# Moving two copies of a decoder step, the spread of a bias table and the carry-over of a convolution state, from the convolution into the first feed-forward block

## The chip, the core and the metric

The kernel runs on one core of one Trainium2 chip. The metric is device time in microseconds (us); of several runs the median is given. The profile is one execution taken by the hardware profiler; its times count from the first instruction of the span.

## What is computed

One inference step of a two-layer decoder: 512 prompt tokens and 64 sample tokens (8 sequences of 8), width 1024. Layer 0 mixes tokens with a convolution module, layer 1 with sliding-window attention that has a relative-position bias. Both layers then run a causal feed-forward block (width 2816, with a 3-tap convolution inside) and add a gated per-layer embedding.

```python
def _conv_module(xn, hist, ...):
    u = xn @ w_pw1 + b_pw1
    a, g = jnp.split(u, 2, axis=-1)
    u = a * jax.nn.sigmoid(g)
    uh = jnp.concatenate([hist.astype(u.dtype), u], axis=1)
    c = _dwconv_valid(uh, w_dw) + b_dw
    c = jax.nn.silu(_layernorm(c, ln_g, ln_b))
    return c @ w_pw2 + b_pw2, uh[:, -(CONV_K - 1):]
def _rel_bias(dist, table):
    vals = table[_t5_bucket(dist)].astype(jnp.float32)
    return jnp.moveaxis(vals, -1, 0).reshape(N_KV_HEADS, GROUP, *dist.shape)
```

Two small things in this matter here. The new convolution state of the 8 sample sequences is the last 30 rows of `uh`: 22 old rows, copied unchanged from `state_conv` (output `conv_old`, 704 KB), and 8 new ones. The bias of head h between two positions depends on their distance alone, so one row of 383 numbers for each of 16 heads holds all of it.

## The kernel before

The core goes through four stages in order: `conv_stage`, `ffn_stage(0)`, `att_stage`, `ffn_stage(1)`. Activations lie as 128 features by tokens. Tokens are handled in two parts, part 0 of 256 columns and part 1 of 320 (256 prompt, 64 sample). Every product is made of three matrix multiplications, high by high, high by low and low by high (`mm3`, lines 175 to 177). So each weight block of 128 x 1024 (512 KB) is loaded by a DMA of the SP queue into one of 3 `raw` buffers (line 216), rounded by ScalarE into `wh` (line 163), and VectorE, or for a few blocks GpSimd, makes the rest `wl` (line 166 or 223). In the feed-forward stage 8 pairs `wh`/`wl` are live (4 in `wp`, 4 in `w2`), and `ensure` runs up to 4 blocks ahead of use.

The order of work in the convolution is written out in the string `CONV`: `aM,P` is the first projection of block M, part P (`pw1`); `mM` regroups its result through DRAM (`regroup`, DMAs `d_u` and `x`), `cM,G` is a group of taps of the depthwise convolution as 18 multiplications (`taps`, lines 584 and 585), `bM` brings the result back through DRAM (`ungroup`, DMAs `d_c` and `h`), `oM` is the sample part on GpSimd (`taps_smp`, line 611 on). A group of taps has its own weights, 576 KB, loaded into one of two `traw` buffers (line 565, the first 12 on the GpSimd queue, the other 20 on SP's), rounded by ScalarE into `th`, the rest made by VectorE into `tl`. A scheduler may move instructions a little on each engine; those under `keep` stay in the order of the program.

`bias_table` makes the 16 rows of 383 numbers in the SBUF tile `ng` (16 partitions) and returns a function that spreads them: each row is written 128 times to `d_bias` in DRAM (16 x 128 x 383 numbers, 3064 KB), so that attention can later read it with a step of 382 and get the bias by distance (`bias_rows`, line 451). Entry `B` of `CONV`, in the middle of the convolution, calls this function (line 443) and issues the copy of `conv_old` (line 641), both on the GpSimd queue:

```python
elif kind == "B":
    bias_out()
    keep(nc.gpsimd.dma_start(out=o["conv_old"], in_=a["state_conv"][0][:, 8:30, :]))
```

In `ffn_stage` the list of `ffn_order` alternates `A` (up-projection of pair x, part 0), `B` (part 1) and the down-projections `DA`, `DB` of groups of pairs. In `up`, part 1 uses GpSimd for three small copies (lines 726, 727 and `stash`, line 732); products go to one of 6 PSUM banks (`bank`), which ScalarE and VectorE empty.

Of the kernel before, what the change touches and what calls it, by code (L numbers as in the profile page):

```python
# [9 lines left out]
F32 = mybir.dt.float32  # L10
# [7 lines left out]
P = 128  # L18
# [9 lines left out]
QSB = 5  # L28
LBUF = 4
CONV = """  # L30
X0 a0,0 X1 a1,0 a2,0 a0,1 m0 a1,1 m1 a3,0 o0 a2,1 m2 c0,0 a4,0 c0,1 c0,2 o1 a3,1 c0,3 b0 m3 c1,0 a5,0 c1,1 c1,2 o2 a4,1 c1,3 b1 m4 c2,0 a6,0 c2,1 c2,2 B
o3 a5,1 c2,3 b2 m5 c3,0 a7,0 c3,1 c3,2 o4 a6,1 c3,3 b3 m6 c4,0 c4,1 i0,0 o5 a7,1 c4,2 m7 c4,3 b4 c5,0 i0,1 c5,1 c5,2 P c5,3 b5 o6 c6,0 p0,0 c6,1 c6,2 c6,3
b6 o7 c7,0 i1,0 c7,1 c7,2 c7,3 b7 p0,1 i1,1 L0 p1,0 L1 M0 p1,1 w0,0 w1,0 M1 w0,1 w2,0 w1,1 w3,0 n0 w2,1 r0 w3,1 n1 r1
"""
# [121 lines left out]
class Trunk:  # L156
# [273 lines left out]
    def bias_table(self, sp):  # L430

        nc, a = self.nc, self.a
        tab = sp.tile([32, 16], F32, tag="tab", name="tab", bufs=1)
        nc.scalar.dma_start(out=tab, in_=a["rel_bias"])
        oh = sp.tile([32, 384], F32, tag="pst", name="oh")
        nc.scalar.dma_start(out=oh, in_=a["c_onehot"])
        ng = sp.tile([16, 384], F32, tag="ng", name="ng", bufs=1)
        nc.scalar.dma_start(out=ng, in_=a["c_neg"])
        ps = self.bank("bps", st=True)
        self.T.matmul(ps[0:16, :384], lhsT=tab, rhs=oh, start=True, stop=True)  # L440
        self.V.tensor_tensor(out=ng, in0=ps[0:16, :384], in1=ng, op=ALU.add)
        self.d_bias = self.drp.tile([16, P, 383], F32, name="d_bias")
        return lambda: self.tc.keep_in_program_order(nc.gpsimd.dma_start(out=self.d_bias, in_=ng[:, 0:383].unsqueeze(1).to_broadcast([16, P, 383])))

    def bias_rows(self, out, h0, nh, nq, ns):

# [36 lines left out]
    def conv_stage(self):  # L483
        nc, tc, a, o = self.nc, self.tc, self.a, self.o
# [13 lines left out]
        self.d_pp = {(l, p): self.drp.tile([P, KD, PN[p]], F32, name=f"d_pp{l}{p}") for l in range(2) for p in PARTS}  # L498
        with tc.tile_pool(name="w2c", bufs=2) as w2, tc.tile_pool(name="cvp", bufs=2) as sp:
            self.phase("conv", w2)  # L500
            bias_out = self.bias_table(sp)
            cc = self.h
            us, norms = {}, {}
            keep = tc.keep_in_program_order
            x = sp.tile([P, 4, 136], F32, tag="x", name="x", bufs=1)
# [7 lines left out]
            def pw1(m, part):  # L513

                n = PN[part]
                if part == 0:
                    us[m] = sp.tile([P, 816], F32, tag="u", name="u", bufs=UB)
                    keep(nc.sync.dma_start(out=us[m][:, 512:], in_=a["sc"][m]))
                u = us[m]
                wa, wg = self.wcols(("pw1", m, 0)), self.wcols(("pw1", m, 1))  # L520
                pg = self.bank("pg")
                self.lin(pg[:, :n], wg, part)
                pa = self.bank("pa")
                self.lin(pa[:, :n], wa, part)
                sg = sp.tile([P, 320], F32, tag="sg", name="sg")
                self.V.tensor_tensor(out=sg[:, :n], in0=pg[:, :n], in1=self.Rx[part], op=ALU.mult)
                self.V.tensor_tensor(out=pa[:, :n], in0=pa[:, :n], in1=self.Rx[part], op=ALU.mult)
                self.sig = self.A.activation(out=sg[:, :n], in_=sg[:, :n], func=AF.Sigmoid, bias=self.col["b_pw1"][:, 8 + m:9 + m], scale=1.0)
                ba = self.col["b_pw1"][:, m:m + 1]
                uq = u[:, 0:512].rearrange("p (r q) -> p q r", r=4)[:, part * 64:part * 64 + 64]  # L530
                q4 = lambda t: t[:, 0:256].rearrange("p (q r) -> p q r", r=4)
                self.V.scalar_tensor_tensor(out=uq, in0=q4(pa), scalar=ba, in1=q4(sg), op0=ALU.add, op1=ALU.mult)
                if part:
                    self.done(("pw1", m, 0), ("pw1", m, 1))
                    self.V.scalar_tensor_tensor(out=smp(u, 30, 8), in0=pa[:, 256:320].rearrange("p (b t) -> p b t", b=8), scalar=ba, in1=sg[:, 256:320].rearrange("p (b t) -> p b t", b=8), op0=ALU.add, op1=ALU.mult)
# [3 lines left out]
            def u_out(i):  # L539
                keep(nc.gpsimd.tensor_copy(out=ucat[:, i, 0:32].rearrange("p (r q) -> p r q", r=4), in_=us[i][:, 0:512].rearrange("p (r q) -> p r q", r=4)[:, :, 120:128]))  # L540
                keep(nc.gpsimd.tensor_copy(out=ucat[:, i, 32:96].rearrange("p (b t) -> p b t", b=8), in_=smp(us[i], 30, 8)))
                if i == KD - 1:
                    keep(nc.gpsimd.dma_start(out=o["conv_new"], in_=ucat))
# [47 lines left out]
            def ungroup(m):  # L591

                v = vs.pop(m)
                for r in range(4):
                    nc.sync.dma_start(out=d_c[m][:, :, r].rearrange("g c j -> c g j"), in_=v[32 * r:32 * r + 32])
                dv = d_c[m].rearrange("g c r j -> (g c) r j")
                for part in PARTS:
                    nc.sync.dma_start(out=cc[part][:, m, 0:256].rearrange("p (r j) -> p r j", r=4), in_=dv[:, :, part * 64:part * 64 + 64])
# [23 lines left out]
            for e in CONV.split():  # L622
                kind, v = e[0], [int(d) for d in e[1:].split(",") if d]
                if kind == "X":
                    self.norm_x(v[0], sp)
                elif kind == "a":
                    pw1(*v)
                elif kind == "s":
                    pass
                elif kind == "o":  # L630
                    taps_smp(*v)
                    u_out(*v)
                elif kind == "m":
                    regroup(*v)
                elif kind == "c":
                    taps(*v)
                elif kind == "b":
                    ungroup(*v)
                elif kind == "B":
                    bias_out()  # L640
                    keep(nc.gpsimd.dma_start(out=o["conv_old"], in_=a["state_conv"][0][:, 8:30, :]))
                elif kind == "P":
                    dm = self.smp.tile([P, 1], F32, tag="rs_t", name="dm")
                    self.after(self.A.activation(out=dm, in_=self.zero[:, 0:1], func=AF.Silu), self.sig)
                elif kind == "L":
                    norms[v[0]] = self.ln_y(part_c(v[0]), v[0], sp)
                elif kind == "M":
                    self.ln_apply(part_c(v[0]), v[0], norms.pop(v[0]), sp)
                    self.load_x(v[0], 0)
                    self.load_x(v[0], 4)  # L650
                elif kind == "i":
                    self.proj_in(*v, sp)
                elif kind == "p":
                    self.proj(*v, sp)
                elif kind == "w":
                    self.pw2(*v)
                elif kind == "n":
                    norms[v[0]] = self.norm_y(v[0])
                elif kind == "r":
                    self.norm_apply(v[0], self.bcast_tok(norms.pop(v[0]), v[0]), self.col["g_ffn0"])  # L660
# [132 lines left out]
    def ffn_stage(self, l):  # L793
        nc, tc = self.nc, self.tc
        with tc.tile_pool(name=f"w2f{l}", bufs=4) as w2, tc.tile_pool(name=f"fp{l}", bufs=2) as fp:
            self.fp = fp
            self.phase("ffn", w2)
            self.ft, self.Rp = {}, {}
            self.sf = fp.tile([P, 704], F32, tag="sf", name="sf", bufs=1)
            self.halo = fp.tile([P, 44, 2], F32, tag="halo", name="halo", bufs=1)  # L800
            self.stash = fp.tile([P, 9, 2, 44], F32, tag="stash", name="stash", bufs=1)
            nc.sync.dma_start(out=self.sf, in_=self.a["sf"][l])
            for i, (kind, x) in enumerate(ffn_order()):
                if kind == "A":
                    self.up(l, x, 0)
                elif kind == "B":
                    self.up(l, x, 1)
                else:
                    part = 0 if kind == "DA" else 1
                    self.down(l, x, part)  # L810
                    if x == len(GROUPS) - 1:
                        self.Rp[part] = self.rows(self.norm_y(part), part, fp, "Rp")
            nc.gpsimd.dma_start(out=self.o["ffn_new"][l], in_=self.stash)
            hook = self.sq_acc if l == 0 else self.y_out
            for c in range(5):
                if c < 4:
                    self.ple(l, c, 0, hook)
                if c:
                    self.ple(l, c - 1, 1, hook)
                if c == 3 and l == 0:  # L820
                    self.kv_norm(0)
# [497 lines left out]
```

## Time and profile before

| what | us |
|---|---|
| median of 3 runs | 1550.09 (1550.01 to 1555.15) |
| the profiled execution | 1548.81 |
| its span, first to last instruction | 1547.0 |
| busy TensorE (PE) | 1465.6 (95%) |
| busy VectorE (DVE) | 1025.7 (66%) |
| busy ScalarE (ACT) | 725.0 (47%) |
| busy GpSimd (POOL) | 321.5 (21%) |
| mean granted TensorE clock | 0.967 |

The time of an execution is its span and the 1.8 us around it. Where TensorE is busy nearly all the time, time is lost only where it stands still or runs at a lower clock. So the views are read by stage: first the slices of the span, then the waits of TensorE in the slice where it is idle, then what the engine waited for, back to its DMA. PE busy is not PE at its peak, since the ends of multiplications are modelled.

### The profile page before, as it was taken

What the parts mean: (1) busy time and instruction counts of PE and PEld (TensorE: products, weight loads), DVE (VectorE), ACT (ScalarE), POOL (GpSimd) and SP (SyncE); (2) the same over time, 40 slices, a digit from 0 to 9 for tenths busy, and PEclk for the clock granted to TensorE, in tenths of its full rate; (3) what the DMA queues carried; (4) which work ended last, traced back from release to release, by engine and by line L of the source; (5) the groups of instructions that cost most, each with busy time, mean ns of one, the idle gap of its engine ahead of it and who ended that gap; (6) DMA issues with size and microseconds to landing.
All of it is one profiled execution on the core that took longest, in us unless ns stands there. A gap on an engine that the chain in (4) does not pass through costs nothing.

```text
span 1547.0 us, 27840 instructions
## 1 busy us (share of the span) xinstructions
PE 1465.6 (95%) x10739; PEld 1439.0 (93%) x10739; DVE 1025.7 (66%) x2325; ACT 725.0 (47%) x1578; POOL 321.5 (21%) x450
## 2 busy tenths in 40 slices
PE   8995689799999999999999988999999999999998
PEld 7995688799999999999999987798999999999998
DVE  7675373958765656565777899957856656464784
ACT  5332253724543434343555677743633525252551
POOL 2595160002210111111001232423211111111100
PEclk7998779899999999999999999999999999999999
DMA  7358766523332222323234222215222313131412
GB/s 269 108 170 142 218 216 196 200 87 99 96 110 69 83 87 78 96 69 96 80 113 140 63 78 87 59 42 160 83 82 69 96 55 110 56 110 56 139 52 72
DMA packets 68772, 165.79 MB, mean 107 GB/s; under 512 B 15200, under 2 KB 31024, under 8 KB 68592
## 3 DMA queue, kind: packets, MB, share of 16 engines
q1 hardware_dynamic: 64608, 146.76, 30.7%
q0 software_dynamic: 3760, 16.67, 4.5%
q8 instruction: 84, 1.38, 0.4%
q10 hardware_dynamic: 272, 0.60, 0.1%
q14 instruction: 48, 0.39, 0.1%
HBM read 147.99 MB, written 18.69 MB: 108 GB/s over the span
## 4 chain that ended last, share of the span: by engine, by line
PE 82%; DVE 7%; DMA 5%; ACT 3%; issue 1%; SPq 1%; POOL 1%; DVEq 0%; ACTq 0%; POOLq 0%
PE up L176 12%; PE up L177 12%; PE up L175 12%; PE dn L177 6%; PE dn L176 6%; PE dn L175 6%; DMA traw<-in_tw_dram 3%; PE plg L177 2%; PE plg L176 2%; PE plg L175 2%; PE cps L584 2%; DVE tl L166 1%; PE p L175 1%; PE p L176 1%; PE p L177 1%
## 5 line engine op out<-in xcount | busy, mean ns | idle before, releaser
L176 PE MATMUL up<-hn,wh 128*128 128x256 f32 (+1 forms) x1408 | 416.3, 297 | 3.3 <-DVE hn L166 3.3
L177 PE MATMUL up<-hn,wl 128*128 128x256 f32 (+1 forms) x1408 | 414.9, 296 | 1.1 <-DVE wl L166 1.1
L175 PE MATMUL up<-hn,wh 128*128 128x256 f32 (+1 forms) x1408 | 410.4, 296 | 1.0 <-ACT hn L163 1.0
L163 ACT CAST wh<-raw 128x1024 fp32r<-128x1024 f32 x196 | 203.2, 1050 | 291.1 <-PE up L176 181.7
L166 DVE TENSOR_TENSOR wl<-raw,wh 128x1024 fp32r<-128x1024 f32 x173 | 221.8, 1289 | 156.2 <-ACT wh L163 150.1
L176 PEld LDWEIGHTS up<-hn,wh 128*128 128x128 f32 x1408 | 267.2, 190 | 4.1 <-DVE hn L166 3.8
L177 PEld LDWEIGHTS up<-hn,wl 128*128 128x128 f32 x1408 | 267.0, 190 | 1.5 <-DVE wl L166 1.3
L175 PEld LDWEIGHTS up<-hn,wh 128*128 128x128 f32 x1408 | 265.1, 190 | 1.4 <-ACT hn L163 1.4
L177 PE MATMUL dn<-fh,wl 128*128 128x320 f32 (+1 forms) x704 | 208.2, 296 | 0.0
L175 PE MATMUL dn<-fh,wh 128*128 128x320 f32 (+1 forms) x704 | 207.5, 295 | 0.0
L176 PE MATMUL dn<-fl,wh 128*128 128x320 f32 (+1 forms) x704 | 207.4, 295 | 0.0
L732 POOL COPY stash<-ue 128x18 f32<-128x18 f32 x88 | 72.5, 826 | 540.7 <-ACT ue L729 539.3
L762 DVE TENSOR_TENSOR h<-dn,h 128x256 f32<-128x256 f32 (+1 forms) x192 | 87.6, 456 | 99.7 <-PE dn L177 99.3
L177 PEld LDWEIGHTS dn<-fh,wl 128*128 128x128 f32 x704 | 132.9, 189 | 0.0
L175 PEld LDWEIGHTS dn<-fh,wh 128*128 128x128 f32 x704 | 132.7, 189 | 0.0
L176 PEld LDWEIGHTS dn<-fl,wh 128*128 128x128 f32 x704 | 132.5, 188 | 0.0
L584 PE MATMUL cps<-xx,th 128*128 128x256 f32 x288 | 78.8, 363 | 32.9 <-ACT th L163 32.9
L584 PEld LDWEIGHTS cps<-xx,th 128*128 128x128 f32 x288 | 61.0, 212 | 34.2 <-ACT th L163 34.2
L223 POOL TENSOR_TENSOR wl<-raw,wh 128x1024 fp32r<-128x1024 f32 x23 | 55.8, 2436 | 151.5 <-ACT wh L163 133.9
L166 DVE TENSOR_TENSOR tl<-traw,th 128x1152 fp32r<-128x1152 f32 x32 | 55.2, 1725 | 39.9 <-ACT th L163 37.8
L585 PE MATMUL cps<-xx,tl 128*128 128x128 f32 x288 | 69.4, 242 | 8.4 <-DVE tl L166 8.4
L177 PE MATMUL plg<-hn,wl 128*128 128x256 f32 (+1 forms) x256 | 76.1, 297 | 0.0
(245 smaller groups left out, 3340.4 us busy)
## 6 DMA issues: line engine op xcount, KB each, us to landing
raw<-in_w_dram SPq DMA_DIRECT2D x196, 512.0 KB, 3.7
traw<-in_tw_dram SPq DMA_DIRECT2D x20, 576.0 KB, 4.2
traw<-in_tw_dram POOLq DMA_DIRECT2D x12, 576.0 KB, 4.9
bias<-d_bias SPq DMA_DIRECT2D x8, 512.0 KB, 4.0
d_bias<-ng POOLq DMA_DIRECT2D x1, 3064.0 KB, 35.3
h<-in_x_dram SPq DMA_DIRECT2D x4, 640.0 KB, 6.8
d_pp<-pst SPq DMA_DIRECT2D x8, 320.0 KB, 3.0
pp<-d_pp SPq DMA_DIRECT2D x8, 320.0 KB, 3.4
```

What stands on the lines that cost most here:

```text
L163: return self.A.copy(out=out, in_=in_)
L166: self.V.tensor_tensor(out=out, in0=in_, in1=hi.bitcast(F32), op=ALU.subtract)
L175: mm(out, lhsT=wh, rhs=xh, start=start, stop=False)
L176: mm(out, lhsT=wh, rhs=xl, start=False, stop=False)
L177: mm(out, lhsT=wl, rhs=xh, start=False, stop=stop)
L223: nc.gpsimd.tensor_tensor(out=l, in0=raw, in1=h.bitcast(F32), op=ALU.subtract)
L584: self.T.matmul(ps[:, 0:2 * P], lhsT=h[:, w], rhs=z[:, :, g, d:d + P], start=d == 0, stop=False)
L585: self.T.matmul(ps[:, 0:P], lhsT=l[:, w], rhs=z[:, 0, g, d:d + P], start=False, stop=d == nd - 1)
L732: nc.gpsimd.tensor_copy(out=self.stash[:, :, :, blk], in_=tail)
L762: self.V.tensor_tensor(out=self.h[part][:, m], in0=ps[:, :n], in1=self.h[part][:, m], op=ALU.add)
```

## The change

The spread and the copy leave `CONV` (entry `B` goes) and are issued by `late_copies`, in the first feed-forward block right after `B` of pair 6. Since `ng` is a tile of the convolution's pool, `bias_table` now writes it at once to a new DRAM tile `d_ext` (24 KB, ScalarE's queue), and the spread reads its rows from there, DRAM to DRAM.

```diff
 CONV = """
-X0 a0,0 X1 a1,0 a2,0 a0,1 m0 a1,1 m1 a3,0 o0 a2,1 m2 c0,0 a4,0 c0,1 c0,2 o1 a3,1 c0,3 b0 m3 c1,0 a5,0 c1,1 c1,2 o2 a4,1 c1,3 b1 m4 c2,0 a6,0 c2,1 c2,2 B
+X0 a0,0 X1 a1,0 a2,0 a0,1 m0 a1,1 m1 a3,0 o0 a2,1 m2 c0,0 a4,0 c0,1 c0,2 o1 a3,1 c0,3 b0 m3 c1,0 a5,0 c1,1 c1,2 o2 a4,1 c1,3 b1 m4 c2,0 a6,0 c2,1 c2,2
...
         self.d_bias = self.drp.tile([16, P, 383], F32, name="d_bias")
-        return lambda: self.tc.keep_in_program_order(nc.gpsimd.dma_start(out=self.d_bias, in_=ng[:, 0:383].unsqueeze(1).to_broadcast([16, P, 383])))
+        self.d_ext = self.drp.tile([16, 384], F32, name="d_ext")
+        nc.scalar.dma_start(out=self.d_ext, in_=ng)
+
+    def late_copies(self):
+
+        nc, keep = self.nc, self.tc.keep_in_program_order
+        keep(nc.gpsimd.dma_start(out=self.d_bias, in_=self.d_ext[:, 0:383].unsqueeze(1).to_broadcast([16, P, 383])))
+        keep(nc.gpsimd.dma_start(out=self.o["conv_old"], in_=self.a["state_conv"][0][:, 8:30, :]))
...
-            bias_out = self.bias_table(sp)
+            self.bias_table(sp)
...
-                elif kind == "B":
-                    bias_out()
-                    keep(nc.gpsimd.dma_start(out=o["conv_old"], in_=a["state_conv"][0][:, 8:30, :]))
...
                 elif kind == "B":
                     self.up(l, x, 1)
+                    if l == 0 and x == 6:
+                        self.late_copies()
```

The lines below the edits move down by up to 7: line 565 of before is 572 of the change, 611 is 618, 732 is 736.

What it moves on the engines, at three places. First the GpSimd queue in the middle of the convolution, during the sample taps of block 2 (`pr` and `acc` are the products and their sum, `ucat` collects the new state). Before:

```order
L611 TENSOR_TENSOR pr<-u,cols 128x64x7
L565 DMA traw<-in_tw_dram 128x1152
L443 DMA d_bias<-ng 2048x1x383
L641 DMA out_conv_old_dram<-in_state_conv_dram 8x2x11264
L613 TENSOR_TENSOR acc<-acc,pr 128x64x7
L540 COPY ucat<-u 128x32
```

and with the change:

```order
L618 TENSOR_TENSOR pr<-u,cols 128x64x7
L572 DMA traw<-in_tw_dram 128x1152
L620 TENSOR_TENSOR acc<-acc,pr 128x64x7
L547 COPY ucat<-u 128x32
L548 COPY ucat<-u 128x64
```

The two issues are gone, and nothing takes their place; the spread is 2048 rows of 383 numbers.

Second the same queue in the first feed-forward block, with the change:

```order
L731 COPY ue<-halo 128x2
L736 COPY stash<-ue 128x18
L449 DMA d_bias<-d_ext 2048x1x383
L450 DMA out_conv_old_dram<-in_state_conv_dram 8x2x11264
L730 COPY ue<-sf 128x8x2
```

The two issues stand behind the 14th copy to `stash` (pair 6, the second of its two), ahead of the small copies of pair 7.

Third ScalarE at the start of the convolution, before

```order
L163 CAST th<-traw 128x1152
L323 ACTIVATE hn_95<-h_93,cols 128x256 x4
L163 CAST th<-traw 128x1152
L163 CAST wh<-raw 128x1024 x2
L323 ACTIVATE hn_97<-h_94,cols 128x320
```

and with the change

```order
L163 CAST th<-traw 128x1152
L323 ACTIVATE hn_95<-h_93,cols 128x256 x4
L163 CAST th<-traw 128x1152
L444 DMA d_ext<-ng 16x384
L163 CAST wh<-raw 128x1024 x2
L323 ACTIVATE hn_97<-h_94,cols 128x320
```

The new write of `d_ext` stands ahead of two roundings of weights; it has to wait for VectorE's sum `ng` (line 441). Apart from these, the scheduler puts a few instructions of the convolution in another order; the largest such move on SP's queue brings two loads of tap weights (`traw`) ahead of a `d_u`, four `d_c` and four `x`.

## Rows read from the trace of the kernel before

**Rows 1.** Work by stretch: us busy (count) of each engine, granted clock, DMA share, GB/s.

```profile
100.00:125.00 25.00, 22.36 (x163) 22.17 (x164) 21.47 (x23) 9.67 (x14) 21.16 (x17) 0.93 0.63 183
138.00:166.30 28.30, 0.93 (x8) 0.78 (x7) 2.37 (x5) 0.95 (x3) 8.11 (x7) 0.60 0.99 168
167.47:170.50 3.03, 3.03 (x14) 3.03 (x15) 3.03 (x3) 1.50 (x2) 1.02 (x1) 0.50 0.44 90
460.00:500.00 40.00, 40.00 (x306) 40.00 (x305) 24.02 (x46) 14.06 (x30) 3.67 (x9) 1.00 0.25 82
```

**Rows 2.** Waits in 130 to 170 us: who for whom, total us, times, longest.

```profile
PE cps L584 <- ACT th L163: 28.5, 1, 28.5
ACT th L163 <- DMA traw<-in_tw_dram: 18.2, 3, 15.5
```

**Rows 3.** Timeline of the SP queue: start us, us until the last is issued, DMA.

```profile
127.76 4.21 SPq L518 DMA_DIRECT2D u<-in_sc_dram  x1
132.14 8.96 SPq L598 DMA_DIRECT2D h<-d_c  x2
141.28 13.96 SPq L565 DMA_DIRECT2D traw<-in_tw_dram  x2
```

**Rows 4.** Timeline of the GpSimd queue.

```profile
125.51 1.07 POOL L443 DMA_DIRECT2D d_bias<-ng  x1
126.56 0.58 POOL L641 DMA_DIRECT2D out_conv_old_dram<-in_state_conv_dram  x1
```

**Rows 5.** DMA queues in 140 to 160 us: packets, MB, share of 16 engines.

```profile
q0 software_dynamic: 447, 2.12, 96.7%
q1 hardware_dynamic: 451, 0.26, 4.2%
```

**Rows 6.** DMA issues of the whole span: count, KB each, median us to landing.

```profile
raw<-in_w_dram SPq DMA_DIRECT2D x196, 512.0 KB, 3.7
traw<-in_tw_dram SPq DMA_DIRECT2D x20, 576.0 KB, 4.2
d_bias<-ng POOLq DMA_DIRECT2D x1, 3064.0 KB, 35.3
h<-d_c SPq DMA_DIRECT2D x16, 128.0 KB, 3.8
out_k_old_dram<-in_cache_k_dram POOLq DMA_DIRECT2D x1, 960.0 KB, 8.6
out_conv_old_dram<-in_state_conv_dram POOLq DMA_DIRECT2D x1, 704.0 KB, 37.5
```

**Rows 7.** Timelines of ScalarE and VectorE after the gap: a tap's rounding and rest.

```profile
166.26 1.15 ACT L163 CAST th<-traw 128x1152 fp32r<-128x1152 f32 x1 [15.47 <-DMA traw<-in_tw_dram]
167.44 1.36 DVE L166 TENSOR_TENSOR tl<-traw,th 128x1152 fp32r<-128x1152 f32 x1 [15.96 <-ACT th L163]
```

**Rows 8.** GpSimd in the feed-forward block: the 14th copy to the stash.

```profile
481.28 0.89 POOL L732 COPY stash<-ue 128x18 f32<-128x18 f32 x1 [0.81 <-ACT ue L729]
```

**Rows 9.** DMA queue of the weight loads, feed-forward, 456 to 500 us.

```profile
q1 hardware_dynamic: 1008, 3.67, 26.1%
```

**Rows 10.** Timeline of the weight loads and roundings in the feed-forward block.

```profile
492.18 2.60 SPq L216 DMA_DIRECT2D raw<-in_w_dram  x3
489.50 2.95 ACT L163 CAST wh<-raw 128x1024 fp32r<-128x1024 f32 x3 [4.14 <-PE dn L176]
499.58 1.05 ACT L163 CAST wh<-raw 128x1024 fp32r<-128x1024 f32 x1 [0.87 <-PE up L176]
503.10 1.05 ACT L163 CAST wh<-raw 128x1024 fp32r<-128x1024 f32 x1 [1.32 <-PE up L176]
```

**Rows 11.** The start: ScalarE's roundings, VectorE's `ng`, TensorE's first product with them.

```profile
13.32 2.07 ACT L163 CAST wh<-raw 128x1024 fp32r<-128x1024 f32 x2
15.04 0.54 DVE L441 TENSOR_TENSOR ng<-bps,ng 16x384 f32<-16x384 f32 x1 [1.24 <-PE bps L440]
19.22 0.56 PE L175 MATMUL pa<-hn,wh 128*128 128x256 f32 x1
```

## The prediction, made before the change was run

> **What bounds the kernel now.** TensorE is busy 95% of the span and in the feed-forward blocks all of it, 40.00 of 40.00 us at full clock in the stretch from 460 us [rows 1]. A change off TensorE's path can therefore only win where TensorE stands still, and the stretch to look at is 138.00 to 166.30 us: 0.93 us of work in 28.30, while the DMA engines are 0.99 busy [rows 1]. The waits of that stretch tell what ended it: one wait of 28.5 us of the tap multiplications for ScalarE's rounding of a tap block, and ScalarE in turn waited for the load of that block, `traw` [rows 2]. So I read the queue that issued this load. SP has it only at 141.28 us, behind a `u` load whose issue took 4.21 us and two `h` loads that took 8.96, and then the two tap loads 13.96 [rows 3]. All this begins right after GpSimd issued the spread at 125.51 us and the copy of the state at 126.56; the issue of the copy took no more than 0.58 us [rows 4].
>
> What the two do to the others is in the count of packets. In 140 to 160 us the GpSimd queue (q0) moved 447 packets and had 96.7% of the sixteen engines' time; SP's queue (q1) moved 451 packets, nearly the same number, but only 0.26 MB [rows 5]. So the engines serve the two queues about packet by packet. A packet of q0 is 2.12 MB / 447 = 4.7 KB, three rows of 1,532 bytes, and takes 0.967 x 16 x 20 us / 447 = 0.69 us; each small packet of the convolution's regrouping waits for one of these. The spread landed after 35.3 us and the copy after 37.5 [rows 6], about the length of the hold-up.
>
> **The change part by part.** *Taking the two transfers out of the convolution.* The wait of 28.5 us [rows 2] is the term. After it TensorE runs 3.03 us at clock 0.50, the lower of its two levels, 1.2 GHz [rows 1]; at 2.4 GHz this work takes 1.5 us. Upper bound: 28.5 + 1.5 = 30.0 us. What comes in the wait's place? Without the hold-up SP reaches the tap load not at 141.28 but, from 127.76 on, three issues later, at about 129 us. It lands 4.2 us later [rows 6], is rounded in 1.15 and its rest made in 1.36 [rows 7], so it is ready at 129 + 4.2 + 1.15 + 1.36 = 136 us, before TensorE asks for it at 138.9 (the end of the wait, 167.47, less 28.5). The first tap is no longer late. The next ones have two buffers and about 6.7 us from load to ready, beside projections of the same kind as in 100 to 125 us, where TensorE lost 25.00 - 22.36 = 2.6 us [rows 1]. I take 2.5 us of such waits in the stretch's place. Lower bound of this term: half of the wait comes back, since the small transfers of the regrouping, drained during the gap, are now due beside the tap loads; I take the other end because the stretch before the gap has the same mixture and a DMA share of only 0.63 [rows 1]. Term: -27.5 us, bounds -31 and -14 (-31 if nothing takes the wait's place and the two tap loads that moved up on SP save another 1 us).
>
> *The two issues on GpSimd, 1.07 + 0.58 us [rows 4], in the feed-forward block.* They come after the 14th stash copy, which starts at 481.28 us [rows 8], and delay the small copies of pair 7. TensorE doesn't wait for GpSimd in that stretch, it is 100% busy [rows 1], and its results can stay in five other PSUM banks. Cost 0; without that cover 1.7 us.
>
> *The transfers themselves, beside the weight loads.* This is the term that could cost. In the 44 us from 456 us the weight queue moved 3.67 MB, seven loads of 512 KB, one each 6.3 us, in packets of 0.261 x 16 x 44 us / 1008 = 0.18 us [rows 9]. A load is 128 rows of 4 KB, 8 per engine. The spread is 2048 / 3 = 683 packets, 43 per engine. If every weight packet waits for one of the spread's, whose time is R, the hold-up lasts at most 43 x (R + 0.18) us, and in it 43 / 8 = 5.4 weight loads arrive. The block needs one each 6.3 us, 34 us for 5.4, so the loads fall behind by **43 x (R + 0.18) - 34 us**. With 0.69 us [rows 5] this is 3.4 us. What hides it: three loads are issued at 492.18 and the first two are rounded at 499.58 and 503.10 [rows 10], 7.4 and up to 10.9 us later, where landing takes 3.7 [rows 6]; and when ScalarE does wait, TensorE goes on into the five other banks, 3.5 us each (the distance of the two roundings, both released by a product [rows 10]), so for some 17 us. Cost 0. Bounds of R, since no row shows a spread with its source in DRAM: below, a DRAM-to-DRAM copy in large pieces, 960 KB in 8.6 us [rows 6], by which the spread's 3064 KB take 27 us, R = 0.64; above, twice the 0.69 us, 1.4 us, in case that reading the same few rows in DRAM again and again costs as much as writing them. I take 0.69, the same destination in the same pieces. At the upper bound the loads fall behind by 43 x 1.58 - 34 = 34 us, less 17 of cover: 17 us of stall.
>
> Here a rule of the Trainium skill speaks against the change. "DMA: Bandwidth & Descriptors", section "Issuing engines are not separate DMA queues", says that transfers run on the same sixteen engines and interleave, whichever engine issued them; by it the moved transfer takes its time from the weight loads in full, which is the first rival below. Another page speaks for it: "SBUF — State Buffer", section "Door 1: The DMA port swizzle", says that the rate of a DMA depends on how many of sixteen ports its partitions reach. The 16 partitions of `ng` reach four of them, which by the page's 435 GB/s would be an estimate of 109 GB/s; 2.12 MB in 20 us [rows 5] are 106, so the trace agrees. By that page a source in DRAM would be rid of this limit, and that rival less likely than I put it; no run here shows it yet. By either page the term here stays at 0, since the bound of 3.4 us of lag is covered.
>
> *The write of `d_ext` at the start.* ScalarE must wait for `ng`, ready at 15.04 + 0.54 = 15.6 us, before it rounds the two blocks that it rounded from 13.32 on: with an issue of some 0.5 us it is about 2.7 us later. TensorE's first product with them stands at 19.22 us [rows 11], after the delayed end of the first one, 16.1 + 1.05 = 17.1. Cost 0, at most 2 us.
>
> **Sum.** 1548.81 - 27.5 = 1521.3 us for the profiled execution, which lies 1.3 us below the median of the runs (1550.09). So 1522.6, say **1523 us**, and 1519 to 1530 by the small terms (-31 at one end; the start's 2 us, GpSimd's 1.7 and as many waits in the gap's place once more at the other).
>
> **The rivals.** *The feed-forward block starves.* The wait moves instead of going: weight loads fall behind, ScalarE stands before a rounding with the emptying of PSUM queued behind it, and TensorE runs out of banks. For it: TensorE has no idle time there that could absorb anything. Against: the weight loads go in large packets, 8 per engine, while the `h` loads of the convolution that took 3.8 us in the median [rows 6] were in the queue that SP could hardly get through [rows 3]. Price: 43 x (R + 0.18) - 51 us. It eats the whole gain at R = 1.65 us and makes the kernel slower by over 0.5% (7.8 us, about what a measurement of this kernel can tell from no change) from R = 1.83 on; with R = 2.0 it is 1523 + 43 = 1566 us. With R = 1.4 it gives 1540.
>
> *Half of the wait comes back in the convolution.* The work after the gap found its small transfers done; now tap loads, regrouping and weights share the engines. Then 1550 - 14 = 1536 us, within 1530 to 1542. Against it stands the stretch before the gap, busy to 89% with the same mixture [rows 1].
>
> *The gap was not the transfers' doing.* The tap load would be late anyway by SP's order, and the time stays near 1549 (that the two issues really are gone from there, the order of the GpSimd queue shows). Against it: the same load lands in 4.2 us elsewhere, the issue stood there 13.96 us [rows 3, 6].
>
> **How the numbers follow.** Forecast 0.74; half comes back 0.14; starvation 0.07, of which 0.02 still faster, 0.02 within 0.5% and 0.03 slower; no effect 0.05. Faster by over 0.5% (below 1542.3): 0.74 + 0.14 + 0.02 = 0.90. Within: 0.05 + 0.02 = 0.07. Slower: 0.03. The range goes from 1516, the bound of -31 (1519) and 3 us more, should the tap loads that moved up also take away the 2.6 us of waits of a later stretch, to 1538, which takes in more than half of the second case and the first rival up to R = 1.35: about 0.85.
>
> **What would show it.** Right: no wait of TensorE over 4 us between 125 and 165 us, clock 1.00 through it, the tap loads at 4 to 5 us, and the end of the convolution earlier by about 27 us; then weight loads of 7 to 9 us landing for about 37 us after the 14th stash copy, with TensorE at 100%. Wrong: new waits of tap multiplications for `traw` that add up to over 8 us, or waits of `up` or `dn` multiplications for PSUM or for `wh` in the first feed-forward block.

## The result, and the profile after

| | before | with the change |
|---|---|---|
| median, us | 1552.45 (1550.01 to 1555.15, 4 runs: the three of the table before and one more) | 1531.23 (1530.30 to 1533.98, 4 runs) |
| the profiled execution, us | 1548.81 | 1530.30 |
| its span, us | 1547.0 | 1528.5 |
| busy TensorE, us | 1465.6 (95%) | 1468.1 (96%) |
| mean granted TensorE clock | 0.967 | 0.968 |

The ratio is 0.9866, with a 95% interval of 0.984 to 0.9891: faster by 1.3%. The forecast was 1523 us with a range of 1516 to 1538, so the time lies in the range, 8 us above the forecast. It also lies outside the forecast's own 1519 to 1530 and inside what the second rival gave (1530 to 1542), which is what most of the study is about.

Both programs run the same 10,739 multiplications in nearly the same order, so the start of a multiplication with a given number, read from both traces, tells where the difference of 18.5 us arises (times in us; the last column is experiment 8 below):

| number, stage | before | change | difference | e8 |
|---|---|---|---|---|
| 900, taps, before the gap | 137.83 | 137.83 | 0.0 | 137.84 |
| 950, projection behind the gap | 174.06 | 143.76 | -30.3 | 143.77 |
| 1050 | 186.94 | 156.77 | -30.2 | 157.48 |
| 1100 | 194.07 | 170.54 | -23.5 | 164.55 |
| 1600, end of the convolution | 280.37 | 257.06 | -23.3 | 251.26 |
| 2100, first feed-forward block | 363.00 | 343.68 | -19.3 | 334.21 |
| 4400, behind the moved transfers | 668.60 | 649.28 | -19.3 | 639.82 |
| 10738, the last | 1541.82 | 1523.37 | -18.5 | 1512.93 |

So the gap went in full, 30.3 us; 11.0 us came back before the feed-forward block; and there, where the two transfers now are, nothing was lost. Another 0.9 us went later, around the attention.

Work by stretch with the change (columns as in [rows 1]; the third and fourth answer to its last row):

```profile
125.00:165.00 40.00, 37.22 (x294) 37.02 (x293) 24.41 (x32) 14.23 (x22) 22.09 (x15) 1.00 0.61 186
165.00:200.00 35.00, 26.45 (x159) 25.53 (x160) 27.40 (x30) 17.72 (x26) 25.37 (x16) 0.74 0.69 221
440.00:480.00 40.00, 40.00 (x306) 40.00 (x305) 24.34 (x46) 14.26 (x31) 5.25 (x11) 1.00 0.53 117
480.00:520.00 40.00, 40.00 (x311) 40.00 (x310) 25.34 (x48) 20.09 (x48) 8.99 (x18) 1.00 0.51 149
```

Where there were 0.93 us of TensorE work in 28.30, there are 37.22 in 40. TensorE stays at 40.00 of 40.00 beside the moved transfers, although the DMA share doubles from 0.25 to 0.51 to 0.53. But the stretch from 165 us has only 26.45 us of work in 35.

The waits in 130 to 170 us, which answer to [rows 2] (who for whom, total us, times, longest):

```profile
PE cps L591 <- ACT th L163: 6.6, 1, 6.6
...
ACT pT L163 <- DMA praw<-in_p_dram: 3.4, 1, 3.4
ACT wh L163 <- DMA raw<-in_w_dram: 1.8, 1, 1.8
```

In place of one wait of 28.5 us there is one of 6.6, from 162.22 to 168.83 us, of a tap multiplication for ScalarE's rounding (tap block 17, counted from 0). This time the rounding `th` is not late by its own load: it stands behind two other roundings, of `pT` and `wh`. ScalarE's timeline there (start us, us, ..., idle before and releaser):

```profile
157.13 1.16 ACT L163 CAST th<-traw 128x1152 fp32r<-128x1152 f32 x1 [4.89 <-DMA traw<-in_tw_dram]
...
164.26 0.62 ACT L163 CAST pT<-praw 128x512 fp32r<-128x512 f32 x1 [3.38 <-DMA praw<-in_p_dram]
166.68 1.04 ACT L163 CAST wh<-raw 128x1024 fp32r<-128x1024 f32 x1 [1.79 <-DMA raw<-in_w_dram]
167.63 1.15 ACT L163 CAST th<-traw 128x1152 fp32r<-128x1152 f32 x1
```

`pT` and `wh` wait for loads that SP issued late. Its timeline:

```profile
151.01 1.20 SPq L605 DMA_DIRECT2D h<-d_c  x2
152.25 0.62 SPq L560 DMA_DIRECT2D x<-d_u  x1
152.91 7.13 SPq L572 DMA_DIRECT2D traw<-in_tw_dram  x3
160.09 0.43 SPq L464 DMA_DIRECT2D praw<-in_p_dram  x1
160.56 0.91 SPq L216 DMA_DIRECT2D raw<-in_w_dram  x2
```

SP needs from 152.91 to 160.04 us for three tap loads, because there are two `traw` buffers and a load must stand until VectorE has read the block two before it (the last of the three is block 18's, and VectorE is done with block 16 at 159.69 us). The load of the projection (`praw`) and of the weights (`raw`), in order behind them, get out only at 160.09 and 160.56, and two of ScalarE's roundings follow them. The kernel before has the same order, on SP and on ScalarE:

```profile
172.69 11.38 SPq L565 DMA_DIRECT2D traw<-in_tw_dram  x4
184.12 0.42 SPq L457 DMA_DIRECT2D praw<-in_p_dram  x1
184.60 0.90 SPq L216 DMA_DIRECT2D raw<-in_w_dram  x2
```

```profile
189.64 0.62 ACT L163 CAST pT<-praw 128x512 fp32r<-128x512 f32 x1 [3.75 <-DMA praw<-in_p_dram]
190.96 1.05 ACT L163 CAST wh<-raw 128x1024 fp32r<-128x1024 f32 x1 [0.71 <-DMA raw<-in_w_dram]
191.92 1.14 ACT L163 CAST th<-traw 128x1152 fp32r<-128x1152 f32 x1
```

There TensorE waited only 0.73 us for this `th`, because the loads ran further ahead. Block 18's was issued 8.6 us before TensorE asked for block 17 (183.75 and 192.39 us); with the change it is 2.5 us (159.71 and 162.22). The head start is lost at block 16's load: its buffer is free at 148.79 us, but from 146.27 to 152.87 us SP issues ten small transfers of the regrouping (`x`, `d_c`, `h`). In the kernel before the four `d_c` among them went during the gap, from 162.05 us, and the rest by 172.65 us, so that block 16's load waited for its buffer alone (176.62, issue at 176.65).

In the feed-forward block, the issues on GpSimd, and the landing of the moved transfers, which answer to [rows 4] and [rows 6]:

```profile
461.95 0.89 POOL L736 COPY stash<-ue 128x18 f32<-128x18 f32 x1 [1.11 <-ACT ue L733]
462.76 1.06 POOL L449 DMA_DIRECT2D d_bias<-d_ext  x1
463.81 0.59 POOL L450 DMA_DIRECT2D out_conv_old_dram<-in_state_conv_dram  x1
```

```profile
d_bias<-d_ext POOLq DMA_DIRECT2D x1, 3064.0 KB, 23.7
...
out_conv_old_dram<-in_state_conv_dram POOLq DMA_DIRECT2D x1, 704.0 KB, 26.6
```

From DRAM the spread takes 23.7 us where it took 35.3 from `ng`. The weight loads issued beside it suffer all the same. The DMA queues from the issue of the first of three of them, at 472.86 us, to 480.11 us:

```profile
q0 software_dynamic: 278, 1.28, 105.2%
issues: line engine op xcount, KB each, median us to landing
raw<-in_w_dram SPq DMA_DIRECT2D x3, 512.0 KB, 17.2
```

For 7.25 us not one packet of the weight queue (q1) moved; 278 of the spread did, 17.4 per engine, 1.052 x 16 x 7.25 / 278 = 0.44 us each. Then the two queues move about equal numbers of packets, as they did in [rows 5]; from 481 to 484 us:

```profile
q1 hardware_dynamic: 85, 0.35, 58.1%
q0 software_dynamic: 82, 0.29, 46.4%
```

ScalarE's roundings of these weights, which answer to [rows 10]:

```profile
470.18 2.95 ACT L163 CAST wh<-raw 128x1024 fp32r<-128x1024 f32 x3 [4.15 <-PE dn L176]
488.59 1.05 ACT L163 CAST wh<-raw 128x1024 fp32r<-128x1024 f32 x1 [9.21 <-DMA raw<-in_w_dram]
491.54 1.05 ACT L163 CAST wh<-raw 128x1024 fp32r<-128x1024 f32 x1 [0.76 <-DMA raw<-in_w_dram]
499.19 1.05 ACT L163 CAST wh<-raw 128x1024 fp32r<-128x1024 f32 x1
```

Before, the rounding behind the group of three came at 499.58 us; 19.33 us earlier that is 480.25, so 488.59 is 8.3 us late. TensorE did not notice.

### The profile page after: what moved, and what is told of

Read it like the earlier page. It is cut to its first block, busy times and chain, and to the rows that moved or that the text cites. A ratio compares the mean times of both kernels' runs of the same rounds, so it can differ in the third digit from the quotient of the medians.

```text
span 1528.5 us, 27837 instructions
## 1 busy us (share of the span) xinstructions
PE 1468.1 (96%) x10739; PEld 1443.5 (94%) x10739; DVE 1027.3 (67%) x2325; ACT 721.8 (47%) x1578; POOL 327.0 (21%) x450
## 4 chain that ended last, share of the span: by engine, by line
PE 81%; DVE 8%; DMA 4%; POOL 3%; ACT 2%; issue 2%; SPq 1%; DVEq 0%; POOLq 0%; ACTq 0%
PE up L176 12%; PE up L177 12%; PE up L175 12%; PE dn L177 6%; PE dn L176 6%; PE dn L175 6%; PE plg L177 2%; PE plg L176 2%; PE plg L175 2%; DMA traw<-in_tw_dram 2%; PE cps L591 1%; POOL pr L618 1%; PE p L175 1%; PE p L176 1%; PE p L177 1%
## 5 line engine op out<-in xcount | busy, mean ns | idle before, releaser
L166 DVE TENSOR_TENSOR tl<-traw,th 128x1152 fp32r<-128x1152 f32 x32 | 58.9, 1841 | 34.8 <-ACT th L163 34.8
L176 PE MATMUL plg<-hn,wh 128*128 128x256 f32 (+1 forms) x256 | 75.9, 296 | 0.0
## 6 DMA issues: line engine op xcount, KB each, us to landing
d_bias<-d_ext POOLq DMA_DIRECT2D x1, 3064.0 KB, 23.7
```

Of the source, the lines that this page charges most:

```text
L166: self.V.tensor_tensor(out=out, in0=in_, in1=hi.bitcast(F32), op=ALU.subtract)
L176: mm(out, lhsT=wh, rhs=xl, start=False, stop=False)
```

## The experiments

The theory after the result: the spread caused the gap, the state's copy hardly; its new source and its new place both count; and the 11 us came back through SP's order behind the gap. Each part was then tried alone. All times are medians beside runs of the kernel before on the same chip.

**1. The copy of the state alone.** `d_bias` keeps entry `B` and its source `ng`.

```diff
 elif kind == "B":
     bias_out()
-    keep(nc.gpsimd.dma_start(out=o["conv_old"], ...))
...
     self.up(l, x, 1)
+    if l == 0 and x == 6: tc.keep_in_program_order(nc.gpsimd.dma_start(out=self.o["conv_old"], ...))
```

> Only the copy of the convolution state goes to the feed-forward block; the spread stays in the convolution with its source in SBUF. Theory (the spread's 43 slow packets per engine, served in turn with SP's, hold up the tap loads): the wait of the tap multiplications shrinks by 0 to 3 us of 28.5, the time is 1 to 4 us below the kernel before. Rival (the copy's pieces of 45 KB block the engines): the wait shrinks by over 10 us, the time by over 8 us.

Measured: 1547.46 us against 1550.95, ratio 0.9969 (0.9954 to 0.9985). The gap shrinks to 25.2 us and stays; the copy alone lands in 7.0 us, so its 37.5 before were the spread's doing.

```profile
PE cps L584 <- ACT th L163: 25.2, 1, 25.2
```

**2. The spread alone.** The change, with the copy left at entry `B`.

```diff
-        keep(nc.gpsimd.dma_start(out=self.o["conv_old"], ...))
...
+                elif kind == "B":
+                    keep(nc.gpsimd.dma_start(out=o["conv_old"], ...))
```

> Only the spread goes to the feed-forward block (source in DRAM); the state copy stays in the convolution. The order on TensorE, ScalarE and SP is that of the change. Theory: the copy alone holds the engines for some 4 us and costs 0 to 4 us, so the time is 1531 to 1535 us. Rival (the copy matters as much as the spread): 10 us or more above the changed kernel.

Measured: 1531.28 us, ratio 0.9867 (0.9837 to 0.9897), the change's own time, with its new wait (6.05 us before the same tap). Once the spread is gone, moving the copy adds nothing that these runs can tell (the interval is 0.3% to either side); beside the spread it was worth the 3 us of experiment 1.

**3. The new source in the old place.** Both transfers at entry `B`, the spread read from `d_ext`.

```diff
+                elif kind == "B":
+                    self.late_copies()
...
-                    if l == 0 and x == 6:
-                        self.late_copies()
```

> Both transfers stay at their old place in the convolution, but the spread reads its rows from DRAM. The order on TensorE and SP is that of the kernel before. Theory (the slow packets came from the 16 partitions as source): the spread lands after some 24 us as in the changed kernel, not 35, and the wait of the tap multiplications is 15 to 20 us: 1539 to 1544 us. Rival (only the place counts, not the source): wait of 28 us, 1550 to 1552 us. Rival two (the order of the convolution's instructions makes the gain): as the kernel before.

Measured: 1538.69 us, ratio 0.9914 (0.9887 to 0.9941). The gap is 15.5 us and the spread lands in 23.2:

```profile
PE cps L591 <- ACT th L163: 15.5, 1, 15.5
```

```profile
d_bias<-d_ext POOLq DMA_DIRECT2D x1, 3064.0 KB, 23.2
```

**4. The old source in the new place.** The 16 rows are loaded back into 16 partitions of a tile in the feed-forward pool, and the spread reads that.

```diff
-        keep(nc.gpsimd.dma_start(out=self.d_bias, in_=self.d_ext[:, 0:383]....))
+        keep(nc.gpsimd.dma_start(out=self.d_bias, in_=self.ng[:, 0:383]....))
...
+            if l == 0:
+                self.ng = fp.tile([16, 384], F32, tag="ng", name="ng2", bufs=1)
+                nc.sync.dma_start(out=self.ng, in_=self.d_ext)
```

> Both transfers in the feed-forward block, but the spread reads the rows from SBUF again (they are loaded back into 16 partitions at the start of the block). Theory: the spread takes 33 to 37 us again, weight loads land after 18 to 30 us, ScalarE's roundings come 8 to 18 us late, and the PSUM banks and the blocks that lie ready hide it: 0 to 3 us above the changed kernel. Rival (the faster source in DRAM is what kept TensorE fed): stall of 8 us or more, 1539 us or more.

Measured: 1539.31 us, ratio 0.9917 (0.9895 to 0.994). My expectation failed. The spread takes 35.5 us again, and after the issue of the first of three weight loads at 473.30 us no weight packet moves for 13.9 us; the queues from 473.3 to 487.2:

```profile
q0 software_dynamic: 296, 1.36, 95.9%
issues: line engine op xcount, KB each, median us to landing
raw<-in_w_dram SPq DMA_DIRECT2D x3, 512.0 KB, 25.7
```

That is 18.5 of the spread's packets per engine, at 0.72 us. ScalarE's roundings:

```profile
495.85 1.05 ACT L163 CAST wh<-raw 128x1024 fp32r<-128x1024 f32 x1 [16.03 <-DMA raw<-in_w_dram]
503.20 1.04 ACT L163 CAST wh<-raw 128x1024 fp32r<-128x1024 f32 x1 [5.15 <-DMA raw<-in_w_dram]
```

By the numbered multiplications this kernel stands 18.9 us ahead of before at number 2100 and 8.4 at number 4400: 10.5 us lost in the feed-forward block. 4.5 us of it are two waits for a PSUM bank that ScalarE, standing before its roundings, had not emptied, and 2.0 are two waits for weights behind them; the rest is mostly work at the lower clock after these waits (granted 0.71 from 505 to 510 us and 0.66 from 525 to 530). The waits of the block, and the work by stretch (TensorE busy 5.78 of 10 us, at a clock of 0.83):

```profile
PE up L175 <- ACT ue L733: 4.5, 2, 4.2
PE dn L175 <- ACT wh L163: 1.1, 1, 1.1
PE dn L177 <- DVE wl L166: 0.9, 1, 0.9
```

```profile
500.00:510.00 10.00, 5.78 (x35) 5.58 (x35) 5.04 (x10) 4.15 (x10) 1.50 (x3) 0.83 0.42 149
```

By the ratios, place alone is worth some 13 us, source alone some 13 us, both together 21.

**5. Three spreads.** Two more, into tiles that nobody reads.

```diff
+        for i in range(2):
+            d = self.drp.tile([16, P, 383], F32, name=f"d_more{i}")
+            keep(nc.gpsimd.dma_start(out=d, in_=self.d_ext[:, 0:383]....))
```

> The change, with the spread of the 16 rows issued three times in a row in the first feed-forward block (the two extra ones into DRAM tiles that nobody reads; the outputs are the same), so about 9.2 MB in place of 3.1. Theory: what a weight load suffers beside the spread is (a) a fixed number of some 17 packets of the spread per engine, already queued, that go before its first packet when the weight queue has been empty, 17 x 0.43 = 7.3 us, and then (b) packet by packet, which at 0.43 + 0.18 = 0.61 us for one of the 8 weight packets per engine is 4.9 us a load, less than the 6.3 us in which the block wants one. So a longer spread only makes more loads late by the same 12 us or so, the three buffers and the PSUM banks still cover it, and TensorE loses little: 1531 to 1535 us, waits of up or dn multiplications in the first feed-forward block under 3 us together. Rival: the lag grows with the bytes, as the prediction's formula has it when loads fall behind steadily; one spread made ScalarE 8.3 us late, three make it 25 us late, over the cover of 17 us: 8 us of stall or more, at least 1539 us.

Measured: 1543.05 us, ratio 0.9949 (0.9932 to 0.9965), with one stall of 8.5 us in the block and 14.2 us lost there in all. The time is the rival's, but the run does not decide: with the extra transfers the scheduler also put three roundings of weights later on ScalarE, behind the emptying of PSUM, so that SP issued the next three loads together, at 498.32, 499.94 and 501.46 us; with the change they went at 490.92, 493.88 and 501.52. What it does show is the hold-up twice in one kernel. The first of three loads issued from 470.88 us saw no weight packet for 6.6 us, 16.4 packets of the spread per engine. From 478 us on packets of both queues moved, 283 and 289 from 480 to 488 us, until the weight queue was empty again at 492. Three loads issued from 498.32 us then met the next spread; from there to 504.53 us:

```profile
q0 software_dynamic: 268, 1.15, 103.7%
```

16.8 packets per engine, and none of the weights'.

**6 to 8. Three ways to take away the wait of 6.6 us.** Two put tap loads on other queues than SP's: those of the blocks 12 to 17 on GpSimd's, or all from 12 on on ScalarE's.

```diff
-                (nc.gpsimd if i < 12 else nc.sync).dma_start(out=raw, in_=a["tw"][i])
+                (nc.gpsimd if i < 18 else nc.sync).dma_start(out=raw, in_=a["tw"][i])
```

> The change, with the tap loads 12 to 17 on GpSimd's queue in place of SP's (before and change have the first 12 there). Theory: the new wait of 6.6 us before tap block 17 is SP's order: SP stands before the load of tap block 17 until its buffer is free (160.09 us), and the projection's and the weights' loads, whose roundings stand ahead of that tap's on ScalarE, are issued only behind it. With the load on another queue they go earlier; the wait falls to under 2 us and the time by 3 to 6 us, to 1525 to 1528 us. Rival: the wait is the work itself (ScalarE's roundings and the DMA engines, busy 0.6 to 0.7 of that stretch), or GpSimd issues the tap loads no earlier because it has its own sample taps ahead of them: the wait stays at 5 us or more or moves to another tap block, and the time at 1530 to 1533 us.

```diff
-                (nc.gpsimd if i < 12 else nc.sync).dma_start(out=raw, in_=a["tw"][i])
+                (nc.gpsimd if i < 12 else nc.scalar).dma_start(out=raw, in_=a["tw"][i])
```

> The change, with the tap loads from 12 on on ScalarE's queue in place of SP's. Theory (SP's order makes the 6.6 us): the wait before tap block 17 falls to under 2 us, since SP is free to issue the projection's and the weights' loads; but ScalarE itself now stands before an issue whose buffer VectorE has not freed, so I expect some of it back in waits for ScalarE: 1526 to 1531 us. Rival (not SP's order): the wait stays at 5 us or more, 1531 us or more.

The third leaves the queues alone and puts the projection's entry two entries later in `CONV`.

```diff
-... b3 m6 c4,0 c4,1 i0,0 o5 a7,1 c4,2 m7 c4,3 b4 c5,0 ...
+... b3 m6 c4,0 c4,1 o5 a7,1 c4,2 m7 c4,3 i0,0 b4 c5,0 ...
```

> The change, with the entry i0,0 of the convolution's order (first part of the mixing projection of block 0, whose weight is loaded as praw and rounded as pT) two entries later, behind the taps c4,3. Theory (ScalarE rounds in its order, and the rounding of tap block 17 stands behind two that wait for loads that SP issued late): one of these roundings falls behind the tap's, so the wait before tap block 17 falls from 6.6 to about 3 us and the time to 1527 to 1530 us. Rival: the other rounding, of a weight block, stands there all the same and its load lands as late, so the wait stays at 5 us or more and the time at 1530 to 1532 us.

| | median, us | ratio to before | wait before tap block 17, us |
|---|---|---|---|
| the change | 1531.23 | 0.9866 (0.984 to 0.9891) | 6.6 |
| 6: taps 12 to 17 on GpSimd's queue | 1523.33 | 0.9823 (0.9808 to 0.9837) | 3.9 |
| 7: taps from 12 on on ScalarE's | 1526.59 | 0.9839 (0.9817 to 0.9861) | under 1 |
| 8: projection later | 1522.22 | 0.9815 (0.9793 to 0.9837) | under 1 |

All three have lower medians than the change; the intervals of 6 and 8 lie clear of the change's, that of 7 overlaps it. The work is the same in all, so the wait came from the order of loads on SP and of roundings on ScalarE, not from the amount of work. In number 6 block 16's load, no longer behind the regrouping, goes out at 146.96 us, and 3.9 us of the wait are left, with `pT` and `wh` still ahead of `th`. (The load before which SP stood was block 18's, which number 6 leaves on SP, not block 17's as its expectation says.) In 7 and 8 `pT` is no longer ahead of this `th`. In 7 `praw` even goes out later than with the change, at 168.81 us, so it did not win in the way expected. Number 6 left more of the wait than I expected and still came out 2 us better. Number 8 won more than I expected, because the scheduler, free of the projection, also moved two `raw` loads ahead of the tap loads, and the rounding of tap block 17 stood behind weights that were already there. ScalarE in experiment 8, against the rows of the change above:

```profile
157.81 1.16 ACT L163 CAST th<-traw 128x1152 fp32r<-128x1152 f32 x1 [4.86 <-DMA traw<-in_tw_dram]
...
159.13 1.04 ACT L163 CAST wh<-raw 128x1024 fp32r<-128x1024 f32 x1
160.99 0.56 ACT L535 ACTIVATE sg<-sg,cols 128x320 f32<-128x320 f32 x1 [0.82 <-DVE sg L533]
161.46 1.03 ACT L163 CAST wh<-raw 128x1024 fp32r<-128x1024 f32 x1
162.40 1.15 ACT L163 CAST th<-traw 128x1152 fp32r<-128x1152 f32 x1
```

The rounding of tap block 17 starts at 162.40 us in place of 167.63. The table above shows the rest: experiment 8 keeps 28.8 of the 30.3 us as far as the feed-forward block, where the change keeps 19.3.

**9 and 10. Both at once, and the control.** Number 9 is the change with edits 6 and 8.

> Both edits that took the wait of 6.6 us before tap block 17 away, in one kernel: the change, with the projection's entry i0,0 two entries later and the tap loads 12 to 17 on GpSimd's queue. Theory: they remove the same wait by two ways, so they do not add up: 1519 to 1524 us, against 1522.2 us with the projection later alone and 1523.3 us with the tap loads alone. Rival: each also takes away waits that the other leaves (3.9 us before tap block 17 is left by the tap loads alone, 3 to 5 us of small waits between 170 and 245 us by either), so they add up in part: below 1519 us.

Measured: 1519.77 us (1516.55 to 1523.53), ratio 0.9786 (0.9762 to 0.9809). It is the lowest median of the study, but its interval overlaps that of number 8; whether the second edit adds anything is not settled.

Number 10 is the kernel before, transfers in place, with edit 8 alone.

> The kernel before, spread and copy where they were, with only the projection's entry i0,0 two entries later. Theory: before, the gap of 28.5 us covers these loads, so the order of the projection is worth nothing there: 1549 to 1553 us, within 0.3% of before, with the gap of 28 us in place; the 9 us that the same edit won on top of the change are then the part of the gap that had come back as a wait. Rival: the order is worth its 9 us with the transfers in place as well, and has nothing to do with the change: 1540 to 1544 us.

Measured: 1549.08 us, ratio 0.9979 (0.9963 to 0.9996), with the gap as it was:

```profile
PE cps L584 <- ACT th L163: 28.8, 1, 28.8
```

The order of the projection is worth 0.2% while the gap covers it, and without the gap 9 us by the medians, 8 by the ratios.

## Why the prediction came out as it did

*The wait of 28.5 us and the cold restart, upper bound 30.0.* Right: 30.3 us are gone at multiplication 950. That the spread and not the copy made the gap is shown by experiments 1 and 2.

*"I take 2.5 us of such waits in the stretch's place."* This step failed. 11.0 us came back between multiplications 950 and 2100, 6.6 of them in one wait. The reason given was that the stretch before the gap has the same mixture and a DMA share of only 0.63. It has not: in 100 to 125 us the tap loads, blocks 8 to 11, go on GpSimd's queue. From block 12 on they stand in SP's order, where block 16's went out late behind the regrouping, the loads of the mixing projection and of the weights stood behind block 18's, and ScalarE rounded in that order. Experiment 6, with the loads 12 to 17 on GpSimd's queue as well, is 7.9 us below the change. The lower bound of the same term had described the first half of this ("the small transfers of the regrouping, drained during the gap, are now due beside the tap loads"), and half of the wait coming back had the chance 0.14; what came back is 11.0 / 30.3, a bit over a third.

The text's own signs say the same. Of those of being right, no wait of TensorE over 4 us between 125 and 165 us failed: the wait of 6.6 us begins at 162.22. The convolution ended 23.3 us earlier and not 27, and the weight loads beside the spread landed after 17.2 us and not 7 to 9; the clock of 1.00 up to 165 us and TensorE at 100% beside the moved transfers came. The sign of being wrong, new waits of tap multiplications over 8 us, was just missed: they are 12.0 + 4.0 us in 125 to 245 us, where before had 32.9 + 4.3, so 16.0 against 8.7 without the gap, 7.3 more.

The rest came later: 2.3 us between numbers 1600 and 1700, in the normalisation behind the convolution, and 1.7 at the entry of the feed-forward block. What causes these was not tried, and they differ from trace to trace. Experiments 4 and 5, with the change's order of multiplications up to there, lost 0.6 and 2.9 us at the first place, and at the second one lost 2.7 and the other won 1.8; in all 12.4 and 9.8 us came back in them. With the order mended, in experiment 8, the 28.8 us left at number 2100 put the term at 1.5 us, and the time at 1522, close to the forecast.

*The two issues on GpSimd.* Right: 1.06 + 0.59 us, with TensorE at 40.00 of 40.00.

*The transfers beside the weight loads, cost 0.* The cost was 0, but by another way than the working said. Three steps of it were off, in different directions. (a) The time of one packet of the spread was 0.44 us and not 0.69, because the source was the limit, not the writing: experiments 3 and 4 separate source from place. (b) "If every weight packet waits for one of the spread's" holds only once the weight queue is running. A queue that had been empty first waited for 16.4 to 18.5 packets of the spread per engine. So ScalarE was 8.3 us late, where packet by packet it would have been on time at 0.44 us (43 x 0.62 = 27 us, less than 34). (c) The cover of 17 us was somewhat too large, and what a stall costs behind it was left out. In experiment 4 the two roundings came at 495.85 and 503.20 us, where 18.9 us before the 499.58 and 503.10 of [rows 10] would be 480.7 and 484.2. TensorE's waits for a bank at these two places are 0.3 and 4.2 us, so 15.2 us of lateness cost nearly nothing, 19.0 us cost 4.5, and the cover was about 14.5 us. The loss of 10.5 us is larger because TensorE then waited 2.0 us more for weights and ran at the lower clock. By the prediction's formula the lag at 0.72 us would be 43 x 0.90 - 34 = 4.7 us and not 19; the first wait of 13.9 us, which it does not have, makes up most of the difference. At 0.72 us, close to the R = 0.69 that the prediction took, the kernel stands at 1539 us: the forecast of no cost came true only because the new source is faster. That was luck.

*The rule of the Trainium skill against the change.* "DMA: Bandwidth & Descriptors", "Issuing engines are not separate DMA queues": the traces agree, the weight loads beside the spread landed after 17.2 us in place of 3.7; it decided nothing here since those loads are early. The same page of the Trainium skill says in "Queues, rings and completion order" that an engine drains a whole packet, typically some 9 to 17 descriptors, from one queue before it turns to the next. If what this profile counts as packets were that page's descriptors, which no run shows, the 16.4 to 18.5 of them would be about one turn at its upper end, and the first wait 17 x 0.69 = 11.7 us at the prediction's own R (an estimate from that page); experiment 4 measured 13.9. But the sharing afterwards does not go by turns of 17: in experiment 4 it is 186 packets of each queue from 488 to 497 us. What makes the first wait stays open.

*The rule for it.* "SBUF — State Buffer", "Door 1: The DMA port swizzle" of the Trainium skill: the rate goes by the ports that the partitions reach. Two pairs of runs fit it: with the source in DRAM the spread took 23.2 against 35.3 us in the convolution, and 23.7 against 35.5 in the feed-forward block. Whether it is the ports or something else about the 16 partitions was not tried, and what limits the spread from DRAM, 3064 KB in 23.7 us, no run shows.

*The write of `d_ext`, 0 to 2 us.* Right: multiplication 900 starts at 137.83 us in both; in the other traces, with the write and without, it lies between 136.4 and 139.5.

*No effect* (0.05) and *starvation* (0.07): neither came. Experiment 4 shows that starvation was nearer than 0.07 for the spread as the prediction priced it.

## What to carry to other kernels

When a long wait goes, list what had been finished during it, queue by queue, and how far ahead of their use the loads behind it went: those transfers are due again, that head start is gone, and the first instruction in order that stands for a buffer holds up all that follow it. Price a bulk transfer beside latency-bound loads by two numbers, the packets that go ahead of a queue that wakes up and the sharing afterwards, and read the time of one packet from a transfer with the same source. A broadcast like this one, 16 rows from 16 partitions, is better read from DRAM.

## What the runs showed of the hardware that was not expected

A DMA queue that had been empty waited for about the same number of the other queue's packets, whatever these took: counted from the issue, 17.4 per engine and 7.25 us (the change), 18.5 and 13.9 us (experiment 4, slower packets), 16.4 and 6.6 us, then 16.8 and 6.2 us (experiment 5, which paid it each time its weight queue woke up beside the spread). Some 1 us of it is a load's own: beside nothing the first packet came 0.96 to 1.00 us after the issue (the kernel before, 444 to 560 us). After that both queues move packets in equal numbers: 85 and 82 in 3 us (the change), 186 and 186 in 9 us (experiment 4), 283 and 289 in 8 us (experiment 5). How the packets of one engine follow each other can't be read, since the records do not name the engine.
